# Dot products of gathered rows handed out one behind each up projection instead of four in a row

## The chip, the cores and the metric

One core of one Trainium2 chip runs the whole program. The metric is the device time of one execution in microseconds (us). The engines are TensorE (PE, matrix products), VectorE (DVE), ScalarE (ACT), GpSimd (POOL) and SyncE (SP). They run side by side, each through a queue of its own, and wait for one another where data or buffers require it.

## What is computed

The kernel is one decoder layer on 512 tokens of width 1024: a combined input projection that feeds differential attention and a convolution module, an output projection, then PEER retrieval of single-neuron experts, then a gated per-layer embedding and a last norm. The change lies in the PEER part. For each token it chooses 8 x 16 of 16384 experts and forms

```python
def chunk(args):
    xc, ec, gc = args
    u = u_tab[ec]
    a = jnp.einsum('cd,ckd->ck', xc, u).astype(jnp.float32)
    h = jax.nn.gelu(a, approximate=False) * gc
    vv = v_tab[ec]
    return jnp.einsum('ck,ckd->cd', h.astype(vv.dtype), vv)
```

## The kernel before, in words

Of the 512 tokens, the first 352 (TU) are computed densely: all 16384 products with the table u by TensorE, gelu, times a gate matrix that is zero for experts not chosen, then times the table v. The other tokens are computed sparsely: their chosen rows of u are gathered from memory, and VectorE forms one dot product for 128 gathered rows at a time.

The stretch around the change is made of three kinds of work, which the program hands out side by side.

**Up projections** (`up`, lines 653 to 674, called through `more(n)`). One of them loads 512 KB of u (`uraw`, four buffers), splits it into `uhi` on ACT (line 658) and `ulo` on DVE (line 659), three buffers each, and runs 24 matmuls of 352 columns (lines 72 to 74). ACT then applies gelu, and SP stores the result of two (`a_spill`).

**Dots** (`sparse_c` and `sparse`, lines 609 to 640, called through `rows(n)`). POOL gathers 128 rows of 4 KB (lines 611 and 629) into `row`, of which there are four buffers, so a gather can start when the dot four places before it is done. DVE multiplies and sums it (lines 613 and 632). Each dot is wrapped in `keep_in_program_order`, which ties it in issue order behind the vector instruction that the program wrote just before it.

**Gate blocks** (the loop over t, b and g, lines 737 to 805). For 16 tokens (GB) at a time they build the gate matrix: a one-hot `o1` on DVE (line 790) or, in every third group, on ACT (lines 785 and 786), a one-hot `o2` and its two scaled copies on DVE (lines 793 to 795, the first scaled copy at 794), 32 short matmuls (line 801) and a copy to `stage` (line 803), which is stored to `g_spill`. Here such a step is called a group; group 0.4 is the fifth of the eight of tile t = 0. There are 22 of them, and a last block of 4 smaller ones for 32 tokens (lines 747 to 770).

In tile 0 the groups also carry **chores**: `next(chores, None)` advances `routeA(1)`, which is vector work on the choice of experts for the next tile (pairs, decode, ending at line 590 with `gTL`). In tiles 1 and 2 there are none left.

A group of the kernel before therefore writes: three up projections, one chore, four dots, `o1`, `o2`. The order in which the engines' queues are filled is not quite that: a planner goes through the program when it is compiled, and puts an instruction that it takes to be ready ahead of one that is not, the earlier written first. The ties of `keep_in_program_order` bind it. `PER` is 3, `ROWS` is 4.

Of the kernel before, what the change touches and what calls it, by code (L numbers as in the profile page):

```python
# [44 lines left out]
FIRST, PER = 16, 3  # L45
CHORE_UPS = 1
ROWS, POOLED = 4, 4
# [12 lines left out]
def hymba_layer(ctx: ExitStack, tc: tile.TileContext, I, out):  # L60
# [3 lines left out]
    def load(dst, src):  # L64
        nc.sync.dma_start(dst, src)
# [408 lines left out]
    def rbank():  # L474
        return psr.tile([128, 512], F32, name="rbank")
# [133 lines left out]
    def sparse_c(j):  # L609
        row = new_row()  # L610
        P.indirect_dma_start(out=row, out_offset=None, in_=I["u"],
                             in_offset=bass.IndirectOffsetOnAxis(ap=cidx[:, j:j + 1], axis=0))
        tc.keep_in_program_order(V.scalar_tensor_tensor(row, row, 1.0, mC, op0=OP.mult, op1=OP.mult, accum_out=ca[:, j:j + 1]))
        if j == NCT - 1:
            A.activation(ca, ca, AF.Gelu)
            for r in range(R):
                rs = slice(r * NCT, r * NCT + NCT)
                V.tensor_tensor(hz[rs, r], ca[rs], cgate[rs], op=OP.mult)
            tp = rbank()
            T.matmul(tp[:, 0:NCT], hz.rearrange("p r j -> p (r j)"), pick, start=True, stop=True)  # L620
            A.activation(hT, tp[:, 0:NCT], AF.Copy)
# [4 lines left out]
    def sparse(i):  # L626
        j = i % 128
        row = new_row()
        P.indirect_dma_start(out=row, out_offset=None, in_=I["u"] if i < 128 else I["v"],  # L629
                             in_offset=bass.IndirectOffsetOnAxis(ap=bidx[:, j:j + 1], axis=0))  # L630
        if i < 128:
            tc.keep_in_program_order(V.scalar_tensor_tensor(row, row, 1.0, mB, op0=OP.mult, op1=OP.mult, accum_out=ba[:, j:j + 1]))  # L632
            if j % 32 == 31:
                js = slice(j - 31, j + 1)
                A.activation(bh[:, js], ba[:, js], AF.Gelu)
                V.tensor_tensor(bh[:, js], bh[:, js], bgate[:, js], op=OP.mult)
        elif j == 0:
            V.tensor_scalar(acc, row, bh[:, 0:1], None, op0=OP.mult)
        else:
            tc.keep_in_program_order(V.scalar_tensor_tensor(acc, row, bh[:, j:j + 1], acc, op0=OP.mult, op1=OP.add))  # L640
# [12 lines left out]
    def up(c):  # L653
        raw = urp.tile([128, KT, 128], F32, name="uraw", bufs=4)
        load(raw, I["ut"][c])
        hi = urp.tile([128, KT, 128], F32R, name="uhi", bufs=3)
        lo = urp.tile([128, KT, 128], F32R, name="ulo", bufs=3)
        A.activation(hi, raw, AF.Copy)  # L658
        (P if c in first[:POOLED] else V).tensor_tensor(lo, raw, f32(hi), op=OP.subtract)  # L659
        ps = rbank() if c in third else psu.tile([128, 512], F32, name="ups")  # L660
        for k in range(KT):
            mm3(ps[:, :TU], hi[:, k], lo[:, k], mTH[:, k, :TU], mTL[:, k, :TU], k == 0, k == KT - 1)
        if c in spilled:
            i = spilled[c]
            av = two(urp, "av", i)
            A.activation(av[:, i % 2], ps[:, :TU], AF.Gelu)  # L666
            if i % 2:
                load(ad[i // 2], av)
        elif c < KEEP:
            ga[c] = two(gap, "ga", c)[:, c % 2]  # L670
            A.activation(ga[c], ps[:, :TU], AF.Gelu)
        else:
            ga[c] = gap.tile([128, TU], F32, name="gu", bufs=1)
            A.activation(ga[c], ps[:, :TU], AF.Gelu)
# [16 lines left out]
    def more(n):  # L691
        nonlocal nu
        while n > 0 and nu < EARLY:
            up(first[nu])
            nu += 1
            n -= 1
# [24 lines left out]
    def rows(n):  # L721
        nonlocal nxt
        while n > 0 and nxt < 128:
            if nxt < 0:
                sparse_c(nxt + NCT)
            else:
                sparse(nxt)
            nxt += 1
            n -= 1
# [7 lines left out]
    for t in range(NA):  # L737
        for _ in chores:
            rows(2)
            more(CHORE_UPS)  # L740
        if t:
            more(4)
        chores = routeA(t + 1) if t + 1 < NA - 1 else iter(())
        for b in range(128 // GT):
            stage = stg.tile([128, NK, GT], F32, name="stage")
            held.append(stage)
            if t * 128 + b * GT >= TU:
                rows(max(0, -nxt))
                for g in range(GT // 8):
                    if g % 2 == 0:  # L750
                        more(PER)
                        rows(ROWS)
                    ts = slice(t * 128 + b * GT + 8 * g - TU, t * 128 + b * GT + 8 * g + 8 - TU)

                    def each(v):
                        return v[:, ts][:, :, None].to_broadcast([128, 8, 128])

                    ib = iota[:, None, :].to_broadcast([128, 8, 128])
                    o1 = gst.tile([128, 8, 128], F32, name="o1", bufs=2)
                    V.tensor_tensor(o1, ib, each(e1F), op=OP.is_equal)  # L760
                    o2 = gst.tile([128, 2, 8, 128], F32, name="o2")[:, 0]
                    V.tensor_tensor(o2, ib, each(e2F), op=OP.is_equal)
                    V.tensor_tensor(o2, o2, each(hT), op=OP.mult)
                    for q in range(2):
                        gb = rbank()
                        for j in range(4):
                            T.matmul(gb[:, j * 128:j * 128 + 128], o2[:, 4 * q + j], o1[:, 4 * q + j], start=True, stop=True)
                        t0 = 8 * g + 4 * q
                        A.activation(stage[:, :, t0:t0 + 4].rearrange("p e t -> p t e"), gb.rearrange("p (t e) -> p t e", t=4), AF.Copy)
                continue  # L770
            for g in range(GT // GB):
                tk = b * GT + g * GB
                more(PER)
                next(chores, None)
                rows(ROWS)
                sh = [128, GB // 2, 128, 2]

                def pairwise(v):
                    return v[:, t, tk:tk + GB].rearrange("p (g i) -> p g i", i=2)[:, :, None, :].to_broadcast(sh)

                it = irep[:, None].to_broadcast(sh)
                if (tk // GB + t * (128 // GB)) % ACT_EVERY == ACT_EVERY - 1:
                    o1 = gst.tile([128, GB, 128], F16, name="o1", bufs=2)
                    for j in range(GB):
                        A.activation(o1[:, j], iota, AF.Abs, bias=ne1[:, t, tk + j:tk + j + 1])
                    A.activation(o1, o1, AF.Relu, bias=ones[:, 0:1], scale=-1.0)
                    pick1 = [o1[:, j] for j in range(GB)]
                else:
                    o1 = gst.tile(sh, F16, name="o1", bufs=2)
                    V.tensor_tensor(o1, it, pairwise(e1T), op=OP.is_equal)  # L790
                    pick1 = [o1[:, j // 2, :, j % 2] for j in range(GB)]
                o2 = gst.tile([128, 2] + sh[1:], F16, name="o2")
                V.tensor_tensor(o2[:, 1], it, pairwise(e2T), op=OP.is_equal)
                V.tensor_tensor(o2[:, 0], o2[:, 1], pairwise(gTH), op=OP.mult)
                V.tensor_tensor(o2[:, 1], o2[:, 1], pairwise(gTL), op=OP.mult)
                for q in range(GB // 4):
                    gb = rbank()
                    for j in range(4):
                        jj = 4 * q + j
                        for i in range(2):  # L800
                            T.matmul(gb[:, j * 128:j * 128 + 128], o2[:, i, jj // 2, :, jj % 2], pick1[jj], start=i == 0, stop=i == 1)  # L801
                    t0 = g * GB + 4 * q
                    A.activation(stage[:, :, t0:t0 + 4].rearrange("p e t -> p t e"),  # L803
                                 gb.rearrange("p (t e) -> p t e", t=4), AF.Copy, scale=1.0 / GS)
            if t * (128 // GT) + b < NG:
                load(gd[t * (128 // GT) + b], stage)
# [230 lines left out]
```

## Time and profile before

| | us |
|---|---|
| median of 3 runs | 1571.63 |
| lowest, highest | 1568.14, 1572.83 |
| profiled execution | 1566.3 |
| its span, first to last instruction | 1564.5 |

Mean granted TensorE clock of the profiled execution: 0.977 of full speed. TensorE is busy for 94% of the span, VectorE 83%, ScalarE 47%, GpSimd 30%. The times of the steps below come from the profiled execution, counted from the start of its span. A row of the timeline gives start, duration, engine, line, operation, output and inputs, shapes and count; in brackets how long the engine had been idle and what ended that. In a row of grouped instructions the two numbers behind the bar are busy us and the mean ns of one, then idle time before them and its releasers.

### The profile page before, as it was taken

The page shows a single profiled execution, that of the slowest core. Times are in us where ns is not written, and L with a number is a line of the kernel's source. Part 1 is how long each engine was busy: PE and PEld are TensorE (multiplying, and loading weights), DVE is VectorE, ACT ScalarE, POOL GpSimd, SP SyncE. Part 2 cuts the span into 40 slices and gives each one's busy share as a digit, 9 for nine tenths or more (in the row PEclk, how much of TensorE's full clock was granted, in tenths as well). Part 3 has the DMA queues.
Part 4 walks back from the last instruction along what each step waited for, and adds up shares of the span by engine and source line. Part 5 has one row for each costly group of instructions (what it writes and reads, how often), then busy time and mean ns, then how long its engine had stood idle before and what let it go on. Part 6 is the DMA issues. An engine that isn't in the chain of part 4 may idle for free. (4 is left out here: it accounts for less than half of the span.)

```text
span 1564.5 us, 22492 instructions
## 1 busy us (share of the span) xinstructions
PE 1468.4 (94%) x7931; PEld 1277.9 (82%) x7931; DVE 1291.2 (83%) x2615; ACT 731.3 (47%) x1248; POOL 474.3 (30%) x348
## 2 busy tenths in 40 slices
PE   8989898998998697999999999999999999998997
PEld 6867476887998697999999888878888888776886
DVE  3999863899999887898888588888988988878756
ACT  4434664222446664777575434434444343334433
POOL 0000102530133331442543234445444444444000
PEclk9999998998999998999999999999999999999999
DMA  7232245401587978999998999999999999999612
GB/s 239 94 109 54 81 174 208 147 1 55 210 279 268 328 284 285 355 369 372 352 383 301 329 365 348 371 356 375 373 374 361 365 345 346 323 349 357 241 52 81
DMA packets 135378, 417.03 MB, mean 267 GB/s; under 512 B 14433, under 2 KB 35553, under 8 KB 133985
## 3 DMA queue, kind: packets, MB, share of 16 engines
q1 hardware_dynamic: 93216, 262.48, 47.2%
q0 software_dynamic: 41472, 151.01, 26.2%
q10 hardware_dynamic: 576, 2.10, 0.3%
q8 instruction: 62, 1.02, 0.3%
q14 instruction: 52, 0.42, 0.1%
HBM read 366.88 MB, written 46.01 MB: 264 GB/s over the span
## 5 line engine op out<-in xcount | busy, mean ns | idle before, releaser
L629 POOL DMA_INDIRECT row<-in_u,bidx x128 | 178.7, 1396 | 311.8 <-DVE row L632 256.6
L629 POOL DMA_INDIRECT row<-in_v,bidx x128 | 191.0, 1492 | 208.5 <-DVE acc L640 180.8
L74 PE MATMUL ups<-mTH,ulo 128*128 128x352 f32 x760 | 247.4, 326 | 7.0 <-DVE ulo L659 7.0
L72 PE MATMUL ups<-mTH,uhi 128*128 128x352 f32 x760 | 248.8, 327 | 4.0 <-ACT av L666 3.0
L73 PE MATMUL ups<-mTL,uhi 128*128 128x352 f32 x760 | 246.7, 325 | 0.0
L845 PE MATMUL y<-vlo,hH 128*128 128x512 f32 x768 | 239.6, 393 | 7.2 <-DVE vlo L69 6.9
L845 PE MATMUL y<-vhi,hH 128*128 128x512 f32 x768 | 238.0, 392 | 7.1 <-ACT hH L68 5.7
L845 PE MATMUL y<-vhi,hL 128*128 128x512 f32 x768 | 237.7, 391 | 0.0
L658 ACT ACTIVATE uhi<-uraw 128x1024 fp32r<-128x1024 f32 x128 | 134.8, 1058 | 192.4 <-PE ups L73 130.3
L632 DVE SCALAR_TENSOR_TENSOR row<-row,mB 128x1024 f32<-128x1024 f32 x128 | 153.3, 1221 | 37.5 <-DMA row<-in_u,bidx 37.3
L659 DVE TENSOR_TENSOR ulo<-uraw,uhi 128x1024 fp32r<-128x1024 f32 x124 | 150.1, 1218 | 39.3 <-ACT uhi L658 36.4
L68 ACT ACTIVATE vhi<-vraw 128x1024 fp32r<-128x1024 f32 x128 | 135.0, 1055 | 99.4 <-PE y L845 74.2
L69 DVE TENSOR_TENSOR vlo<-vraw,vhi 128x1024 fp32r<-128x1024 f32 x128 | 156.1, 1220 | 29.7 <-ACT vhi L68 29.4
L845 PEld LDWEIGHTS y<-vlo,hH 128*128 128x128 f32 x768 | 144.1, 189 | 41.4 <-DVE vlo L69 11.9
L845 PEld LDWEIGHTS y<-vhi,hH 128*128 128x128 f32 x768 | 143.5, 188 | 37.7 <-ACT hH L68 7.3
L845 PEld LDWEIGHTS y<-vhi,hL 128*128 128x128 f32 x768 | 144.2, 189 | 31.4 <-DVE hL L69 1.2
L640 DVE SCALAR_TENSOR_TENSOR acc<-row,bh,acc 128x1024 f32<-128x1024 f32 x127 | 162.2, 1277 | 8.1 <-DMA row<-in_v,bidx 8.0
L74 PEld LDWEIGHTS ups<-mTH,ulo 128*128 128x128 f32 x760 | 144.5, 190 | 8.1 <-DVE ulo L659 8.1
L72 PEld LDWEIGHTS ups<-mTH,uhi 128*128 128x128 f32 x760 | 144.5, 190 | 5.9 <-ACT av L666 3.9
L73 PEld LDWEIGHTS ups<-mTL,uhi 128*128 128x128 f32 x760 | 144.3, 190 | 0.7
L68 ACT ACTIVATE hH<-hf 128x384 fp32r<-128x384 f32 x128 | 66.3, 518 | 121.7 <-PE y L845 74.8
L803 ACT ACTIVATE stage<-rbank 128x512 f32<-128x512 f32 x88 | 88.3, 1173 | 23.1 <-PE rbank L801 23.1
(300 smaller groups left out, 2709.7 us busy)
## 6 DMA issues: line engine op xcount, KB each, us to landing
uraw<-in_ut SPq DMA_DIRECT2D x128, 512.0 KB
vraw<-in_v SPq DMA_DIRECT2D x128, 512.0 KB
g_spill<-stage SPq DMA_DIRECT2D x10, 2048.0 KB
gt<-g_spill SPq DMA_DIRECT2D x16, 1280.0 KB
a_spill<-av SPq DMA_DIRECT2D x52, 352.0 KB
ga<-a_spill SPq DMA_DIRECT2D x52, 352.0 KB
stage<-in_wq SPq DMA_DIRECT2D x16, 512.0 KB
wraw<-in_w_in SPq DMA_DIRECT2D x15, 512.0 KB
```

Source lines behind the costliest of these rows:

```text
L68: A.activation(hi, src, AF.Copy)
L69: V.tensor_tensor(lo, src, f32(hi), op=OP.subtract)
L72: T.matmul(ps, wh, xh, start=first, stop=False)
L73: T.matmul(ps, wh, xl, start=False, stop=False)
L74: T.matmul(ps, wl, xh, start=False, stop=last)
L629: P.indirect_dma_start(out=row, out_offset=None, in_=I["u"] if i < 128 else I["v"], in_offset=bass.IndirectOffsetOnAxis(ap=bidx[:, j:j + 1 ...
L632: tc.keep_in_program_order(V.scalar_tensor_tensor(row, row, 1.0, mB, op0=OP.mult, op1=OP.mult, accum_out=ba[:, j:j + 1]))
L640: tc.keep_in_program_order(V.scalar_tensor_tensor(acc, row, bh[:, j:j + 1], acc, op0=OP.mult, op1=OP.add))
L658: A.activation(hi, raw, AF.Copy)
L659: (P if c in first[:POOLED] else V).tensor_tensor(lo, raw, f32(hi), op=OP.subtract)
L803: A.activation(stage[:, :, t0:t0 + 4].rearrange("p e t -> p t e"), gb.rearrange("p (t e) -> p t e", t=4), AF.Copy, scale=1.0 / GS)
L845: T.matmul(y[t][n], w[:, sl], x[:, n * 512:n * 512 + 512], start=c == 0 and w is hH and x is hi, stop=c == NK - 1 and l)
```

## The change

The loops that hand out the work are altered in two places: in a group each of the three up projections is followed by one dot, and the fourth dot is written behind `o1`. In the last block three dots follow one behind each of the three up projections, and the fourth stands behind the third. The number of up projections, dots and gathers is the same, and so is the order of each kind among itself.

```diff
@@ -748,8 +748,10 @@
                     if g % 2 == 0:
-                        more(PER)
-                        rows(ROWS)
+                        for _ in range(PER):
+                            more(1)
+                            rows(1)
+                        rows(ROWS - PER)
@@ -770,9 +772,10 @@
                 tk = b * GT + g * GB
-                more(PER)
+                for _ in range(PER):
+                    more(1)
+                    rows(1)
                 next(chores, None)
-                rows(ROWS)
                 sh = [128, GB // 2, 128, 2]
@@ -789,6 +792,7 @@
                     V.tensor_tensor(o1, it, pairwise(e1T), op=OP.is_equal)
                     pick1 = [o1[:, j // 2, :, j % 2] for j in range(GB)]
+                rows(ROWS - PER)
                 o2 = gst.tile([128, 2] + sh[1:], F16, name="o2")
```

## Rows read from the trace of the kernel before

**Rows 1.** Stretches: window, length, busy us by engine, clock, DMA share, GB/s.
```profile
core 0: us, PE busy (x) PEld busy (x) DVE busy (x) ACT busy (x) POOL busy (x), PEclk, DMA share, GB/s
466.00:535.00 69.00, 61.86 (x450) 59.70 (x449) 66.69 (x130) 43.36 (x63) 24.82 (x15) 0.98 0.83 292
602.00:845.00 243.00, 243.00 (x1818) 241.18 (x1817) 202.68 (x241) 163.09 (x242) 93.87 (x63) 1.00 0.95 352
845.00:1500.00 655.00, 637.08 (x2991) 539.43 (x2990) 544.87 (x807) 266.67 (x457) 256.60 (x179) 0.99 0.94 342
```
**Rows 2.** Instructions by line, 466 to 602 us: gate matmuls, halves of u, dots.
```profile
L659 DVE TENSOR_TENSOR ulo<-uraw,uhi 128x1024 fp32r<-128x1024 f32 x24 | 28.9, 1219 | 4.3 <-ACT uhi L658 4.3
L613 DVE SCALAR_TENSOR_TENSOR row<-row,mC 128x1024 f32<-128x1024 f32 x22 | 25.9, 1218 | 5.2 <-DMA row<-in_u,cidx 5.2
L801 PE MATMUL rbank<-o,o 128*128 128x128 f16 x238 | 18.4, 238 | 24.8 <-DVE o L794 20.2 <-DVE o L795 4.6
L632 DVE SCALAR_TENSOR_TENSOR row<-row,mB 128x1024 f32<-128x1024 f32 x10 | 12.2, 1224 | 9.0 <-DMA row<-in_u,bidx 8.9
```
**Rows 3.** Timeline, TensorE: the two long waits, groups 0.4 and 0.7.
```profile
547.95 0.61 PE L801 MATMUL rbank<-o,o 128*128 128x128 f16 x4 [10.64 <-DVE o L794]
...
598.38 0.29 PE L801 MATMUL rbank<-o,o 128*128 128x128 f16 x1 [7.23 <-DVE o L794]
```
**Rows 4.** Timeline, VectorE: first and last dot of group 0.4, then its line 794.
```profile
540.50 1.22 DVE L613 SCALAR_TENSOR_TENSOR row<-row,mC 128x1024 f32<-128x1024 f32 x1 [3.91 <-DMA row<-in_u,cidx]
...
545.52 1.23 DVE L613 SCALAR_TENSOR_TENSOR row<-row,mC 128x1024 f32<-128x1024 f32 x1
...
546.67 1.22 DVE L794 TENSOR_TENSOR o<-o,gTH 128x2048 f16<-128x2048 f16 x1
```
**Rows 5.** Timeline, VectorE: last dot of group 0.7, and some of what follows it.
```profile
593.68 1.23 DVE L632 SCALAR_TENSOR_TENSOR row<-row,mB 128x1024 f32<-128x1024 f32 x1 [0.83 <-DMA row<-in_u,bidx]
...
595.97 1.22 DVE L659 TENSOR_TENSOR ulo<-uraw,uhi 128x1024 fp32r<-128x1024 f32 x1
597.10 1.22 DVE L794 TENSOR_TENSOR o<-o,gTH 128x2048 f16<-128x2048 f16 x1
598.24 1.22 DVE L793 TENSOR_TENSOR o<-irep,e2T 128x2048 f16<-128x2048 f16 x1
```
**Rows 6.** Timeline, GpSimd: first, second and fourth gather behind the dots of group 0.3.
```profile
530.53 1.69 POOL L611 DMA_INDIRECT row<-in_u,cidx  x1 [8.96 <-DVE row L613]
532.52 1.99 POOL L611 DMA_INDIRECT row<-in_u,cidx  x1 [0.30 <-issue]
...
536.15 0.94 POOL L611 DMA_INDIRECT row<-in_u,cidx  x1 [0.31 <-issue]
```
**Rows 7.** Timeline, VectorE: last instruction of a chore, first dot behind it, twice.
```profile
513.23 0.28 DVE L563 TENSOR_TENSOR ef<-eq 128x128 f32<-128x128 f16 x1
513.42 1.22 DVE L613 SCALAR_TENSOR_TENSOR row<-row,mC 128x1024 f32<-128x1024 f32 x1
...
565.42 0.28 DVE L590 SCALAR_TENSOR_TENSOR gTL<-rbank,gTH 128x128 f16<-128x128 f32 x1
565.62 1.22 DVE L613 SCALAR_TENSOR_TENSOR row<-row,mC 128x1024 f32<-128x1024 f32 x1
```
**Rows 8.** Stretches, columns as in Rows 1: tile 0's vector work, then later ones.
```profile
466.15:600.51 134.36, 107.21 (x776) 103.33 (x774) 115.79 (x194) 83.28 (x135) 47.66 (x32) 0.92 0.84 299
600.00:612.00 12.00, 11.36 (x81) 11.36 (x82) 10.98 (x10) 5.50 (x7) 0.00 (x0) 0.83 0.89 341
640.00:735.00 95.00, 95.00 (x736) 94.09 (x736) 84.18 (x99) 72.80 (x119) 36.25 (x25) 1.00 0.98 365
```
**Rows 9.** Timeline, ScalarE: line 658 of two projections in a row, paced by TensorE.
```profile
607.93 1.06 ACT L658 ACTIVATE uhi<-uraw 128x1024 fp32r<-128x1024 f32 x1 [2.46 <-PE ups L73]
...
611.77 1.06 ACT L658 ACTIVATE uhi<-uraw 128x1024 fp32r<-128x1024 f32 x1 [2.43 <-PE ups L73]
```
**Rows 10.** Timeline, VectorE: the fourth dot of group 1.3.
```profile
667.48 1.23 DVE L632 SCALAR_TENSOR_TENSOR row<-row,mB 128x1024 f32<-128x1024 f32 x1 [1.95 <-DMA row<-in_u,bidx]
```

## The prediction

> **What bounds the kernel now.** I read the stretches first, because the share of the whole span hides where TensorE is full and where it is not. From 602 to 845 us, tiles 1 and 2 of the gate blocks, TensorE is busy for all 243.00 us at full clock, while VectorE works 202.68 us and has time left [rows 1]. From 845 to 1500 us, the down projections, TensorE is busy for 637.08 of 655 us [rows 1]. Nothing can be won there by an order of vector work. From 466 to 535 us it is the other way: VectorE is busy for 66.69 of 69 us and TensorE for 61.86 [rows 1]. That is tile 0, whose groups also carry the chores.
>
> Next the groups by line from 466 to 602 us: TensorE's gate matmuls stood idle for 24.8 us in front of line 801, waiting for VectorE's scaled one-hots, and in the same time VectorE itself stood idle for 5.2 + 8.9 = 14.1 us in front of dots whose gathered rows had not landed, and for 4.3 us in front of `ulo` [rows 2]. Last the timeline, which puts the two together. Most of TensorE's idle time is two waits, 10.64 us before 547.95 and 7.23 us before 598.38 [rows 3]. In front of the first, VectorE waits 3.91 us for the first row of group 0.4, works off its four dots up to 546.67, and only then makes line 794 [rows 4]. In front of the second it is the same with group 0.7 [rows 5]. So at present TensorE waits for a one-hot, the one-hot stands behind four dots, and the dots wait for gathers.
>
> Why do the dots come so close upon each other? A dot is tied behind the vector instruction written before it, which in tile 0 is the end of a chore. The trace shows the tie: a chore ends with line 563 at 513.23 and the first dot starts at 513.42; another ends with line 590 at 565.42 and the dot starts at 565.62 [rows 7]. A long chore holds four dots back, the dots of the next groups then follow at once, and the gathers between them have no time: the gather that feeds the first dot of group 0.4 started on POOL at 530.53 [rows 6] and its dot could start at 540.50 [rows 4], 10 us later.
>
> **The change, part by part.** *Nothing is added or removed.* The same up projections, dots, gathers and loads are issued; SP's queue (loads of u, stores of gelu and gates) and POOL's queue (the gathers, each order kept) see no new order among their own, only other times. ACT gets no other work. What moves is 88 dots of 22 groups, and 8 of the last block, on VectorE's queue.
>
> *The tie.* Three dots of a group are now tied to the three `ulo` and no longer to the chore; the fourth is tied to `o1`, or to the chore where ACT makes `o1` (2 of the 8 groups of tile 0). As dots started 0.2 us behind their tie [rows 7], the planner takes their rows as landed then, and I expect one dot right behind each `ulo`.
>
> *The gathers.* With four dots in a row 1.15 us apart (540.50 is late, but 545.52 to 546.67 shows the step [rows 4]), POOL starts the four gathers that follow at 530.53 to 536.15, 5.6 us from first to fourth [rows 6], where the dots themselves need 3 x 1.15 = 3.4 us. So the fourth row has 2.2 us less time than the first, and it is at third and fourth dots that the settled stretch still waits, for instance 1.95 us in group 1.3 [rows 10]. Spread out, each gather starts just behind its own dot and has the whole turn of a group, less its own dot. The vector work of tile 0 is 115.79 us for 8 groups [rows 8], so a turn is 115.79 / 8 = 14.5 us, 13.3 without the dot, against the 10 us that the gather above took. The 14.1 us of waits should mostly go. Bounds: all stay (gain 0), all go (gain 14.1). In between, I leave half a microsecond standing in each of the 8 groups, a quarter of the wait in [rows 10], which had 2.2 us less time: 4 us. Gain 10.1 us.
>
> *What the vector queue is then bound by.* From 466.15 to 600.51 us VectorE is busy for 115.79 of 134.36 us [rows 8]; that is its whole work up to the last one-hot of tile 0, and TensorE, busy for 107.21 us there, cannot be ahead of it. So the stretch cannot fall by more than 18.6 us through idle time, and TensorE keeps waits of some 9 us. The 4.3 us in front of `ulo` are not touched, as they come from ACT [rows 2]; bounds 2 to 8, I take 4.3.
>
> *Two instructions of later work* (`ulo` of a projection of tile 1 at 595.97 and line 793 of group 1.0 at 598.24) now stand before the end of tile 0 [rows 5]; they were put there while dots were late. Written later, they go behind: 2 x 1.14 = 2.3 us, if the planner sees it so; bounds 0 and 2.3.
>
> *The clock.* After the second long wait TensorE has a mean granted clock of 0.83 from 600 to 612 us, so part of it at the lower level, 1.2 instead of 2.4 GHz; 12 x 0.17 = 2.0 us of work lost [rows 8]. With shorter waits, as from 466 to 535 (0.98 [rows 1]), half of it should come back: 1.0; bounds 0 and 2.0. The dip after the first wait costs nothing now, since TensorE waits again before 598.38.
>
> *Later stages.* From 602 on TensorE is full, so an earlier start is an earlier end: the gain is carried to the end of the span. The dots in tiles 1 and 2 wait now at no cost, since TensorE works through; what they win there is hidden. In the last block and behind it orders change by chance; +-3 us.
>
> **Sum**: 10.1 + 2.3 + 1.0 = 13.4 us. The profiled execution took 1566.3 (span 1564.5 and 1.8 around it) and would take 1552.9. The median of the runs is 1571.6, 5.3 above it; from that 1558.2, and I predict **1558**. Ends of the unknown: 0 and 14.1 + 2.3 + 2.0 + 2.3 (of the 4.3) = 20.7, with the +-3: 1548 to 1575.
>
> **A rule that speaks against it.** GpSimd's own time for a gather is 0.94 us for one at 536.15 that has little vector work beside it, and 1.69 and 1.99 us for those beside dots [rows 6]. The Trainium skill says why (SBUF — State Buffer, section "SBUF: two separate sides"): GpSimd and VectorE share a pair of ports under an exclusive lock, and a DMA issued from GpSimd gets no descriptors while certain vector instructions hold it. The rows agree in direction. By that rule a VectorE that never pauses makes every gather slow, about 1 us later for half of the 32 gathers of tile 0; if a quarter of these 16 us reaches the vector queue, as 4 of 14.1 do above, the sum is 9.4 instead of 13.4.
>
> **Rivals.** *(A) Transfers are the bound.* The gathers come late not through their order but because memory delivers no faster; then the waits come back one by one in front of single dots, and the end stays. For it: a gather took 10 us [rows 4, 6], and the DMA share is 0.95 in the stretch that follows [rows 1]. Against it: tile 0 moves 134.36 x 299 GB/s = 40.2 MB, and from 640 to 735 us the same mix ran at 365 GB/s with TensorE full [rows 8]; at that rate it takes 110 us, less than the 115.79 of vector work. Time 1571.6, within 3 either way.
>
> *(B) The planner does not hand the dots out.* If it takes the rows as not landed, it fills with one-hots and chores and the dots lump together again, later in the group. For it: it does put other work ahead of what it takes as not ready, as at 598.24 [rows 5]. Against it: [rows 7]. Half the gain at most: 1565.
>
> *(C) Slower: a late row now blocks an `ulo`.* Before, three `ulo` stood in front of the four dots; now the second and third stand behind a dot. ACT makes a new `uhi` every 3.84 us, when TensorE has freed one three projections back [rows 9]; two projections, 7.7 us, are then still to be worked off, less 1.06 and 1.22 for the two halves, 5.4 us of lead, 4.2 behind one dot. A row later than 4.2 us stops TensorE in the stretch where it is full now. The longest wait seen is 3.91 [rows 4], in the settled stretch 1.95 [rows 10]. If the waits grew by half, each of the 14 groups of tiles 1 and 2 would lose about 1.5 us: 21 us slower where tile 0 gains a few, about 1583.
>
> **Chances.** Forecast (gain 8 to 21) 0.60; B 0.14; A 0.17; C 0.09. 0.3% (4.7 us) is about what a measurement of this kernel can tell from no change; B falls on both sides of it, 0.12 faster and 0.02 same. So faster 0.72, same 0.19, slower 0.09. The range leaves out C and a sliver at either end: 1548 to 1573.
>
> **What would show it.** In the profile after, single dots between `ulo` all through tile 0; VectorE's idle time in front of dots from 466 on down from 14.1 to some 4 us; no wait of TensorE at line 801 over 4 us, the sum of them down from 24.8 to about 11; tile 1 starting some 13 us earlier; TensorE still full through tiles 1 and 2. The forecast is wrong if the waits at 801 keep their sum (A, B), or if TensorE shows waits for `ulo` at line 74 between the gate matmuls of tiles 1 and 2 (C).

## The result: slower by 0.8%

| | median us | ratio to before, 95% interval |
|---|---|---|
| before | 1569.64 (7 runs) | |
| changed | 1582.58 (7 runs) | 1.0081 [1.0057, 1.0104] |

I had forecast 1558 and a range up to 1573. The gain that I expected came, and more than twice of it was lost right behind.

The stretches of the changed kernel, tile 0 and then tiles 1 and 2 with the last block (columns as in [rows 1]):

```profile
466.00:592.00 126.00, 111.06 (x790) 107.29 (x788) 117.86 (x215) 82.59 (x135) 50.26 (x32) 0.95 0.87 323
592.00:870.00 278.00, 254.68 (x1848) 251.11 (x1849) 212.37 (x250) 166.46 (x246) 97.56 (x64) 0.96 0.87 319
```

The last one-hots of tile 0 and of tile 2 on VectorE's timeline, in the kernel before (line 795) and in the changed one (line 799):

```profile
599.37 1.22 DVE L795 TENSOR_TENSOR o<-o,gTL 128x2048 f16<-128x2048 f16 x1
808.92 1.22 DVE L795 TENSOR_TENSOR o<-o,gTL 128x2048 f16<-128x2048 f16 x1
```
```profile
591.22 1.22 DVE L799 TENSOR_TENSOR o<-o,gTL 128x2048 f16<-128x2048 f16 x1
833.57 1.22 DVE L799 TENSOR_TENSOR o<-o,gTL 128x2048 f16<-128x2048 f16 x1
```

Tile 0 is over at 592.4 us instead of 600.6. This execution was already 2.2 us late ahead of the change (a vector instruction of line 560 starts at 408.17 us, the same one before at 405.95), so tile 0 itself is 10.4 us shorter. But from 592 to 870 us TensorE, which was busy for all 243.00 us from 602 to 845 [rows 1], is now busy for 254.68 of 278, at a mean clock of 0.96. The last one-hot of tile 2 ends at 834.8 us; before it was 810.1. From the end of tile 0 to there it takes 242.4 us instead of 209.6, 32.8 us more. That stretch before, and in the changed kernel:

```profile
600.60:810.10 209.50, 209.46 (x1582) 207.77 (x1583) 174.64 (x204) 143.23 (x217) 77.47 (x52) 0.99 0.95 351
```
```profile
592.40:834.80 242.40, 219.48 (x1609) 216.04 (x1610) 177.46 (x211) 148.19 (x223) 81.69 (x55) 0.96 0.86 317
```

Who waits shows in the groups by line from 466 to 870 us:

```profile
L74 PE MATMUL ups<-mTH,ulo 128*128 128x352 f32 x424 | 139.9, 331 | 15.2 <-DVE ulo L659 15.2
L632 DVE SCALAR_TENSOR_TENSOR row<-row,mB 128x1024 f32<-128x1024 f32 x74 | 89.7, 1218 | 53.8 <-DMA row<-in_u,bidx 53.7
L74 PE MATMUL rbank<-mTH,ulo 128*128 128x352 f32 x208 | 69.5, 334 | 12.0 <-DVE ulo L659 12.0
L805 PE MATMUL rbank<-o,o 128*128 128x128 f16 x704 | 46.7, 223 | 9.1 <-DVE o L798 5.0 <-DVE o L799 4.1
```

TensorE's waits for one-hots (line 805 here, line 801 before) have gone from 24.8 [rows 2] to 9.1 us. In their place stand 15.2 + 12.0 us in front of line 74, where a projection needs its `ulo`: 4.4 us in tile 0, 22.8 from 592 us on. And VectorE waits 53.7 us for gathered rows.

One such wait, on VectorE's timeline in groups 2.4 and 2.5, with TensorE's wait and the gather concerned behind it:

```profile
809.81 1.22 DVE L659 TENSOR_TENSOR ulo<-uraw,uhi 128x1024 fp32r<-128x1024 f32 x1
810.95 1.22 DVE L632 SCALAR_TENSOR_TENSOR row<-row,mB 128x1024 f32<-128x1024 f32 x1
...
812.09 1.22 DVE L632 SCALAR_TENSOR_TENSOR row<-row,mB 128x1024 f32<-128x1024 f32 x1
...
813.24 1.22 DVE L793 TENSOR_TENSOR o<-irep,e1T 128x2048 f16<-128x2048 f16 x1
814.37 1.21 DVE L797 TENSOR_TENSOR o<-irep,e2T 128x2048 f16<-128x2048 f16 x1
815.51 1.21 DVE L659 TENSOR_TENSOR ulo<-uraw,uhi 128x1024 fp32r<-128x1024 f32 x1
816.64 1.21 DVE L632 SCALAR_TENSOR_TENSOR row<-row,mB 128x1024 f32<-128x1024 f32 x1
...
829.00 1.22 DVE L632 SCALAR_TENSOR_TENSOR row<-row,mB 128x1024 f32<-128x1024 f32 x1 [11.13 <-DMA row<-in_u,bidx]
...
830.15 1.22 DVE L798 TENSOR_TENSOR o<-o,gTH 128x2048 f16<-128x2048 f16 x1
831.29 1.22 DVE L659 TENSOR_TENSOR ulo<-uraw,uhi 128x1024 fp32r<-128x1024 f32 x1
832.42 1.22 DVE L632 SCALAR_TENSOR_TENSOR row<-row,mB 128x1024 f32<-128x1024 f32 x1
```
```profile
832.56 0.66 PE L74 MATMUL ups<-mTH,ulo 128*128 128x352 f32 x1 [7.13 <-DVE ulo L659]
```
```profile
814.43 1.98 POOL L629 DMA_INDIRECT row<-in_u,bidx  x1 [0.31 <-issue]
```

The first `ulo` of group 2.5 is made at 815.51 and its dot follows at 816.64, as written. The next dot, at 829.00, has no `ulo` ahead of it; the second `ulo` comes only at 831.29, with its own dot at 832.42. So the dot at 829.00 is neither the second nor the third. It is the fourth: it is tied to `o1`, made at 813.24, and to nothing else, so the planner put it ahead of the second and third. Its gather is the last of the four on POOL's queue, at 814.43, behind the fourth dot of group 2.4, which gave its buffer free at 813.2. The row is there 14.6 us later; VectorE stands still for 11.13 us, the second `ulo` stands behind that, and TensorE waits 7.13 us.

The trace also records which gather a dot waits for: the gathers signal eight semaphores (counters that an engine can wait for) in turn, and each dot waits for the semaphore of its own gather. By these the dot at 829.00 waits for the gather at 814.43, and the fourth dot overtakes in 9 of the 14 groups of tiles 1 and 2: 1.1, 1.2, 1.4, 1.5, 1.7, 2.0, 2.2, 2.3 and 2.5. These are exactly the groups whose `o1` DVE makes. In the other five ACT makes it, and as there is no chore left, the vector instruction written before the fourth dot is the third dot; tied to that, the fourth dot keeps its turn in all five. The waits in front of these nine dots in the trace are 6.30, 4.15, 4.79, 4.89, 9.84, 0.98, 1.59, 6.15 and 11.13 us, 49.8 of the 51.9 us that VectorE waits for rows after 600 us.

### The profile page after: what moved, and what is told of

Same layout as the page of the kernel before. It is cut to its first block, busy times and chain, and to the rows that moved or that the text cites. A ratio compares the mean times of both kernels' runs of the same rounds, so it can differ in the third digit from the quotient of the medians.

```text
span 1582.9 us, 22483 instructions
## 1 busy us (share of the span) xinstructions
PE 1479.0 (93%) x7931; PEld 1286.9 (81%) x7931; DVE 1290.2 (82%) x2615; ACT 732.5 (46%) x1248; POOL 482.7 (30%) x348
## 5 line engine op out<-in xcount | busy, mean ns | idle before, releaser
L629 POOL DMA_INDIRECT row<-in_u,bidx x128 | 187.0, 1461 | 325.0 <-DVE row L632 287.2
L849 PEld LDWEIGHTS y<-vlo,hH 128*128 128x128 f32 x768 | 143.8, 189 | 44.7 <-DVE vlo L69 15.2
L74 PE MATMUL rbank<-mTH,ulo 128*128 128x352 f32 x264 | 88.5, 335 | 14.7 <-DVE ulo L659 14.7
```

What stands on the lines that cost most here:

```text
L74: T.matmul(ps, wl, xh, start=False, stop=last)
L849: T.matmul(y[t][n], w[:, sl], x[:, n * 512:n * 512 + 512], start=c == 0 and w is hH and x is hi, stop=c == NK - 1 and l)
```

## The experiments

Two theories stood at first. *One*: the fourth dot, tied to `o1` alone, overtakes, and that alone makes the loss. *Two*: any late dot ahead of an `ulo` holds TensorE (this was rival C), so the spread itself is at fault. Each kernel is compared with the kernel before on the same chip.

| kernel | median us | before | ratio, 95% interval |
|---|---|---|---|
| fourth dot behind the third | 1552.9 | 1571.0 | 0.9894 [0.9864, 0.9925] |
| before, only the fourth dot moved | 1619.4 | 1571.0 | 1.0327 [1.0287, 1.0368] |
| change in tile 0 alone | 1551.8 | 1571.0 | 0.9887 [0.9860, 0.9915] |
| change in tiles 1 and 2 alone | 1603.9 | 1571.0 | 1.0234 [1.0188, 1.0279] |
| change, every dot tied to the one before | 1555.7 | 1570.0 | 0.9914 [0.9892, 0.9935] |
| before, the four dots ahead of the chore | 1552.0 | 1570.0 | 0.9892 [0.9865, 0.9920] |

**The fourth dot behind the third.** Against the changed kernel:

```diff
                 for _ in range(PER):
                     more(1)
                     rows(1)
+                rows(ROWS - PER)
                 next(chores, None)
...
-                rows(ROWS - PER)
                 o2 = gst.tile([128, 2] + sh[1:], F16, name="o2")
```

> The change, but the fourth dot of a group is written right behind the third, ahead of chore and o1, so that it is tied to the third dot and can't be issued ahead of the second. Theory 1 (the fourth dot, tied to o1 alone, overtakes the second and third, waits for the gather issued last, and holds the next ulo back): TensorE's waits for ulo at line 74 in tiles 1 and 2 (22.8 us in the changed kernel) fall under 5, tile 0 keeps its gain; the time falls 10 to 15 us under the kernel before, about 1557. Theory 2 (any late dot ahead of an ulo holds TensorE, whichever it is): the waits at line 74 stay over 12 us and the time within 5 us of the changed kernel, 1578 to 1586.

It ran at 1552.9 us. The stretch that answers to the second one above, and the groups by line, 466 to 870 us:

```profile
592.00:870.00 278.00, 277.38 (x2045) 274.97 (x2043) 227.16 (x271) 182.99 (x271) 103.57 (x67) 1.00 0.95 351
```
```profile
L632 DVE SCALAR_TENSOR_TENSOR row<-row,mB 128x1024 f32<-128x1024 f32 x77 | 92.9, 1219 | 14.9 <-DMA row<-in_u,bidx 14.9
L74 PE MATMUL ups<-mTH,ulo 128*128 128x352 f32 x481 | 155.7, 325 | 0.0
L74 PE MATMUL rbank<-mTH,ulo 128*128 128x352 f32 x208 | 67.8, 326 | 0.0
```

TensorE is full again, no wait for `ulo` is left, although three dots still stand between the `ulo`. Single dots wait, but none over 1.95 us after 600 us. That is against theory two.

**Only the fourth dot moved.** Against the kernel before:

```diff
                 next(chores, None)
-                rows(ROWS)
+                rows(PER)
...
+                rows(ROWS - PER)
                 o2 = gst.tile([128, 2] + sh[1:], F16, name="o2")
```

> The kernel before, with three dots in a row as before and only the fourth dot written behind o1. Theory 1: the fourth overtakes the others of its group here too, so TensorE waits for ulo at line 74 in tiles 1 and 2 with nothing spread, 10 to 25 us of it, and the time is 5 to 25 us above the kernel before. Theory 2: no dot has come between the three ulo of a group, so no such waits, and the time is within 5 us of the kernel before.

It ran at 1619.4 us, 48 us slower, twice the upper end of what theory one gave. Nothing is spread here, and yet the same lines wait, 48.4 us of them:

```profile
L74 PE MATMUL ups<-mTH,ulo 128*128 128x352 f32 x383 | 129.6, 340 | 27.0 <-DVE ulo L659 27.0
L632 DVE SCALAR_TENSOR_TENSOR row<-row,mB 128x1024 f32<-128x1024 f32 x66 | 78.2, 1220 | 75.6 <-DMA row<-in_u,bidx 75.6
L74 PE MATMUL rbank<-mTH,ulo 128*128 128x352 f32 x192 | 65.8, 343 | 21.4 <-DVE ulo L659 21.4
```

So the place of the one dot is enough for the loss, and the spread of the other three rather softens it. By the semaphores the same nine fourth dots overtake, and here each goes ahead of all three other dots of its group. Why that is worse than with the spread is not shown.

**The change in tile 0 alone, and in tiles 1 and 2 alone.** The condition in the first kernel is as below; in the second it is `t > 0`. The last block is as before in both.

```diff
                 tk = b * GT + g * GB
+                spread = t == 0
                 for _ in range(PER):
                     more(1)
-                    rows(1)
+                    rows(1 if spread else 0)
                 next(chores, None)
+                rows(0 if spread else ROWS)
...
-                rows(ROWS - PER)
+                rows(ROWS - PER if spread else 0)
```

> The change in tile 0 alone, where the groups carry chores; tiles 1 and 2 and the last block as before. Both theories: tile 0 ends some 9 to 13 us earlier, as in the changed kernel, TensorE is full in tiles 1 and 2, and the time is 8 to 14 us under the kernel before, 1556 to 1562. If the gain of tile 0 was only lent (its dots and transfers put off into the next tiles), the time is within 4 us of the kernel before.

> The change in tiles 1 and 2 alone; tile 0 and the last block as before. Both theories: tile 0 keeps TensorE's waits at line 801 (about 25 us), tiles 1 and 2 add waits for ulo at line 74, 15 to 25 us, and the time is 15 to 25 us above the kernel before, 1585 to 1595. If the waits in tiles 1 and 2 of the changed kernel came from tile 0 ending earlier, they are under 8 us here and the time within 8 us of the kernel before.

Tile 0 alone gives 1551.8 us, 19.2 below the kernel before and more than I had expected; tiles 1 and 2 alone give 1603.9, 32.9 above, also more. The two together are +13.7 us, and the whole change measured 1582.58 - 1569.64 = +12.9. So, as far as the intervals tell, gain and loss stand side by side and neither is lent by the other; with tile 0 as before, tiles 1 and 2 still wait 12.7 + 11.4 us at line 74 after 600 us.

**Every dot tied to the one before.** The changed kernel with its order as written, and one tie more:

```diff
+    def in_turn(ins):
+        tc.keep_in_program_order(ins)
+        if dots:
+            tc.add_manual_dep(ins.ins, dots[-1].ins.name, ...)
+        dots.append(ins)
...
-        tc.keep_in_program_order(V.scalar_tensor_tensor(row, row, 1.0, mC, ...))
+        in_turn(V.scalar_tensor_tensor(row, row, 1.0, mC, ...))
```

(The dependency is of the same kind as that of `keep_in_program_order`, issue order alone; the dots with `mB` are tied likewise.)

> The changed kernel word for word, with one tie more for each dot: behind the dot before it. Nothing is written in another place; a dot can only no longer overtake another. Theory 1 (overtaking alone makes the loss): TensorE's waits for ulo at line 74 in tiles 1 and 2 fall from 26.2 us to under 5, and the time falls 15 to 30 us under the changed kernel, to 1552 to 1567; tile 0 may gain less than in the kernel with the fourth dot behind the third, since a fourth dot tied to a chore holds the next group's dots back. Theory 2 (the fourth dot's place behind o1 costs in itself): waits of over 10 us stay and the time is within 8 us of the changed kernel, 1575 to 1591.

It ran at 1555.7 us, 27 under the changed kernel, with no wait at line 74 after 600 us. The fourth dot is written behind `o1` here as in the change; only the overtaking is gone. Theory one stands, theory two falls in both its forms.

**The four dots ahead of the chore.** That left the gain open: is it the spread, or that the dots are no longer tied to the chores? The kernel before with two lines exchanged, nothing spread:

```diff
                 more(PER)
-                next(chores, None)
                 rows(ROWS)
+                next(chores, None)
```

> The kernel before with one line moved: the four dots in a row are written ahead of the chore instead of behind it, so that they are tied to the third ulo. Nothing is spread. If tile 0's gain comes from the tie to the chores alone, TensorE's waits at line 801 fall as in the kernel changed in tile 0 alone (from 24.8 to about 10 us) and the time is 12 to 20 us under the kernel before, 1551 to 1559. If it comes from the spread, which gives the third and fourth gather more time, VectorE still waits 8 us or more for gathered rows in tile 0, and the time is at most 6 us under the kernel before.

It ran at 1552.0 us, the whole gain. VectorE's timeline shows four dots in a row behind three `ulo`, and the chore (line 538) now behind them:

```profile
497.86 3.48 DVE L659 TENSOR_TENSOR ulo<-uraw,uhi 128x1024 fp32r<-128x1024 f32 x3
501.27 1.21 DVE L613 SCALAR_TENSOR_TENSOR row<-row,mC 128x1024 f32<-128x1024 f32 x1
...
504.71 1.21 DVE L613 SCALAR_TENSOR_TENSOR row<-row,mC 128x1024 f32<-128x1024 f32 x1
...
505.85 0.38 DVE L538 CAST s<-si 128x256 f16<-128x256 uint32 x1
```
```profile
L801 PE MATMUL rbank<-o,o 128*128 128x128 f16 x704 | 47.1, 224 | 10.9 <-DVE o L794 8.4 <-DVE o L795 2.3
```

In tile 0 VectorE waits 2.7 us for rows, TensorE's waits at line 801 fall from 24.8 [rows 2] to 10.9 us. The three kernels at 1552 to 1553 us can't be told apart: handing the dots out one by one adds nothing to putting them ahead of the chore.

## Why the prediction was wrong, point by point

**What bounds the kernel** held. Tile 0 is bound by VectorE, its dots are held by chores and then come too close upon each other, and TensorE pays at the one-hots. Undoing the tie to the chores alone brought 0.9892.

**The gathers.** I left 4 us of VectorE's waits for rows in tile 0; 3.7 were left (1.9 at line 613, 1.8 at line 632). The number was right and the reason only half: I credited the time that the spread gives to the third and fourth gather, but without any spread 2.7 us were left. What matters then, as I read it, is the distance between the dots of one group and those of the next. The 4.3 us in front of `ulo`, which I had called not touched, are gone as well (0.0 us from 466 to 592); in their place VectorE waits 4.1 and 1.2 us for short steps of ACT elsewhere (lines 618 and 569).

**The sum for tile 0** said 13.4. By its end tile 0 was 10.4 us shorter in the changed kernel's profile, which is what the waits for rows lost, 14.1 to 3.7. The term for two later instructions, 2.3, did not come: VectorE works 116.84 us from 468.35 to 592.30 us, no less than the 115.79 before [rows 8], and a one-hot of the next group (line 797, at 590.08) still stands ahead of the last one of tile 0 at 591.22. The clock came back whole and not by half: it is 1.00 from 600 to 612 us, where it was 0.83 [rows 8], so 2.0 us instead of 1.0. In the medians tile 0 alone measured 19.2, but not at the same clock: the median of the mean granted clocks of those executions is 0.978, that of the kernel before 0.971. The two profiled executions, at 0.976 and 0.977, are 11.1 us apart (1555.2 and 1566.3). Where in the span the other executions had the lower clock, no trace shows.

**The tie** is the step that failed. I wrote that the fourth dot is tied to `o1`, and that one dot would follow right behind each `ulo`. In tiles 1 and 2 both are so, the first where DVE makes `o1`. What I did not draw from it: four dots in a row are tied to one another, each behind the dot before, because that is the vector instruction written before it. Handing them out takes these ties away. A dot that hangs on `o1` alone goes wherever `o1` goes, and the planner makes one-hots early, as it did with `o2` in line 793 at 598.24 [rows 5], a row that I had read for something else. POOL's queue kept its order, as I said, but the dots on VectorE's queue no longer had the same order among themselves. In place of one dot behind each `ulo` and nothing else, the runs showed nine overtaking dots with 49.8 us of VectorE's waits, and TensorE waiting 22.8 us behind them; with overtaking alone ruled out the time fell from 1582.6 to 1555.7 us (the kernel before beside them: 1569.6 and 1570.0). That the planner takes rows as landed [rows 7], which I counted in favour of the change, would explain why it places the fourth dot 11 us too early; the runs show the order, not the planner's reason.

**Later stages.** "What they win there is hidden" was right, but I did not ask what they could lose: 32.8 us. Of these, 22.8 are TensorE's waits for `ulo`. The other 10 are time in which it is busy, 219.48 us instead of 209.46, at a mean clock of 0.96 instead of 0.99; how much of them is clock, and how much are matmuls of other work done in the same stretch, these runs don't separate.

**Rival C** had 0.09 and the time that came, 1583, but not the mechanism. It let the waits of all dots grow by half; in fact dots in their turn wait no longer than before, at most 1.95 us in the kernel with the fourth behind the third, and single dots made late by overtaking do the damage. Its point of decision, 4.2 us of lead worked out from [rows 9], held where the lead was whole: waits of 11.13, 9.84, 6.15 and 4.79 us on VectorE show as 7.13, 5.89, 1.47 and 1.06 us on TensorE, 3.7 to 4.7 us hidden, and one of 6.30 us does not show at all. Where a late row follows another before the lead is regained, there is less cover or none: 4.15 us behind the 6.30 cost 2.21, and 4.89 us, 19 us behind the 4.79, cost 5.08, the third longest wait of all.

**Rivals A and B** fell. The same bytes went through 10 us sooner in tile 0, and the planner did hand the dots out. **The rule on the shared ports** (the Trainium skill, SBUF — State Buffer, section "SBUF: two separate sides") agrees with the trace in direction. POOL's gathers of u took 1461 ns on average here, 1396 in the kernel before, and 0.94 us with little vector work beside them [rows 6]:

```profile
L629 POOL DMA_INDIRECT row<-in_u,bidx x128 | 187.0, 1461 | 325.0 <-DVE row L632 287.2
```

Whatever that costs is hidden: with the fourth dot behind the third they took 1455 ns on average, with the four dots ahead of the chore 1402, and the two kernels run alike.

## What to carry to other kernels

An instruction that is held in place only by the one written before it loses its place when something is written between; before splitting a row of such instructions, ask what each piece is tied to then, and how early that thing can be made. In a queue that works in order, waits of an instruction that is off the path are free only as long as the next one on the path has lead, and this lead (here some 4 us, where no earlier wait had used it up) can be worked out beforehand from the buffers. And where work is late because it hangs on a long job, moving it ahead of the job may be all that is needed.

## What the runs showed of the hardware

A gather of 128 rows of 4 KB, put in line at 814.43 us while loads of u and a store of a gate block were under way, landed 14.6 us later; in the kernel before, 10 us had seemed long [rows 4, 6]. And short waits of TensorE came with a lower granted clock around them. In the changed kernel its mean is 0.90 from 695 to 730 us, with a wait of 5.89 us, and 0.90 from 800 to 835, with one of 7.13; between them, from 730 to 800 us, with a single wait of 1.47, it is 1.00.
